# The start of a diffusion layer's first sub-layer: all of its scale and shift as products on TensorE in four column groups, with three ff tiles side by side

## The chip, the core and the metric

One core of a Trainium2 chip runs the whole layer. The metric is device microseconds of one execution; the kernel before takes 2782.91 us, the median of three runs (2781.95 to 2784.03). Engines are named as in the profile: PE is TensorE (PEld its weight loads), DVE is VectorE, ACT is ScalarE, POOL is GpSimd, SP is the engine whose queue issues most loads.

## The reference, cut to what matters

Two streams of 256 tokens (x, and the context ctx) of width 2048 pass a first feed-forward sub-layer, then token mixing, then (x alone) a second feed-forward sub-layer. The change lies in the start of the first sub-layer.

```python
mod   = (silu(c)     @ w_ada + b_ada)     # 9 chunks of 2048: shift, scale, gate of three sub-layers
mod_c = (silu(c_ctx) @ w_ada + b_ada)

def half_ffn(s, m, slot, g, w_up, w_down):
    h = rms_norm(s, g) * (1 + chunk(m, 3 * slot + 1)) + chunk(m, 3 * slot)
    return s + 0.5 * chunk(m, 3 * slot + 2) * swiglu(h, w_up, w_down)

x   = half_ffn(x,   mod,   0, g_norm[0], w_ffn1_up, w_ffn1_down)
ctx = half_ffn(ctx, mod_c, 0, g_norm[0], w_ffn1_up, w_ffn1_down)
```

All is float32. w_ada is 2048 x 18432; chunks 0 and 1 (shift and scale of the first sub-layer) are 33.6 MB of it. w_ffn1_up is 2048 x 11264.

## The kernel before, in words

Activations stand transposed: a d-tile is 128 of the 2048 columns on the partitions, by 256 tokens; there are 16 d-tiles, and x and ctx (the two halves, 0 and 1) lie in pairs of d-tiles. An ff tile is 128 of the 5632 hidden columns; there are 44. For one ff tile TensorE multiplies, over all 16 d-tiles, a gate part and an up part, each as three products of a high and a low part (`mm3`, lines 192 to 194): 96 products of 512 columns (both halves). The weights of a quarter of k (four d-tiles) of one ff tile are one load of 512 KB (`raw`), which ScalarE casts to the high part (`whi`, line 187) and VectorE or GpSimd subtracts to the low part (`wlo`, line 188). `close` forms silu(gate) * up (lines 287, 288).

The operand h of a d-tile needs three things: the inverse rms of both halves (lines 206 to 211, from sums of squares on TensorE, line 228), x scaled by it (GpSimd, line 404), and the d-tile's scale and shift for both conditioning vectors. `wave_h` (lines 393 to 395) then makes the high and low part of h.

Scale and shift come in two ways. `ada_dve` computes one chunk of one d-tile as dot products on VectorE (line 136): two loads of 512 KB (`adaw`), each against both conditioning rows `crow`, which TensorE broadcasts over the partitions beforehand (line 106). `ada_pe` does it on TensorE (line 157): silu(c) and silu(c_ctx) are two weight columns (`cs`), 256 columns of w_ada (scale and shift of one d-tile) are the moving operand, and 16 products add up over k into two rows; the rows are copied (line 159), turned into columns by two small products (line 162), and biased (line 165).

The order of all this is a list written by hand, `PLAN`: P is `ada_pe` of a d-tile (5 of the 16), D is `ada_dve` of one (10, and d-tile 0 ahead of the list), X is a scaling on GpSimd, H is `wave_h`, W and V are the products of one ff tile and one quarter of k, their weights split on GpSimd or VectorE. The k order of the first up projection is the order in which the H stand. Four ff tiles run side by side (`WAVE = 4`, eight PSUM banks). After them each ff tile runs alone, and 1.25 dot products for the remaining modulation (7 chunks) are put behind each quarter (`ada_hook`).

Each engine works through its instructions in a fixed order, which a scheduler makes of the program at build time. Loads go through the SP queue in order, the ones of `ada_dve` in this stretch through ScalarE's queue; a load waits in its queue until its buffer is free.

Of the kernel before, what the change touches and what calls it, by code (L numbers as in the profile page):

```python
# [13 lines left out]
AF = mybir.ActivationFunctionType  # L14
# [15 lines left out]
# order of the first sub-layer's start: P/D modulation of a d-tile on TensorE/VectorE, X normalised pair of  # L30
# d-tiles, H operand of a d-tile, W/V products of (ff tile, quarter of k), its weights split on GpSimd/VectorE
PLAN = (
    "X5 P11 P12 P13 X0 X6 X1 X2 H11 X3 X4 H0 D1 H1 X7 D4 H12 W00 D2 H4 W10 D3 P14 H3 W20 H2 D15 H15 W01 "
    "V11 P5 W21 H13 D7 W30 W31 D6 H6 H5 H14 D9 W02 H7 W12 W32 W22 D8 H8 H9 D10 H10 W03 W13 W33 W23"
).split()
KORD = [int(s[1:]) for s in PLAN if s[0] == "H"]
PE_D = sorted(int(s[1:]) for s in PLAN if s[0] == "P")
WAVE = 4
# [3 lines left out]
# steps of the query projection between those of the long convolution, and of the hyena gate in the attention  # L42
# [11 lines left out]
def hybrid_layer_kernel(ctx: ExitStack, tc: tile.TileContext, a):  # L54
# [39 lines left out]
    # ------------------------------------------------------- inputs, silu(c)  # L94
    cs = cload("cs", (P, KT, 2))
    S.activation(cs, cs, AF.Silu)
    adap_cm = tc.tile_pool(name="adap", bufs=2)
    adap = adap_cm.__enter__()
    crow = [T(adap, (P, D), f"crow{i}", bufs=1) for i in range(2)]
    for b in range(2):  # L100
        for i in range(2):
            r = T(adap, (1, D // 2), "adaw", bufs=4)
            nc.sync.dma_start(r, a["crow"][i : i + 1, b * (D // 2) : (b + 1) * (D // 2)])
            for q in range(2):
                ps = PB()
                PE.matmul(ps, ones[0:1, :], r[:, q * 512 : (q + 1) * 512], start=True, stop=True)
                S.activation(crow[i][:, b * (D // 2) + q * 512 : b * (D // 2) + (q + 1) * 512], ps, AF.Silu)
# [7 lines left out]
    # ------------------------------------------------------- adaLN modulation  # L115
# [8 lines left out]
    def ada_dve(c, d, b, eng=None):  # L124
# [23 lines left out]

    def ada_pe(d):
        """scale and shift of one d-tile of the first sub-layer, as rows on TensorE."""  # L150
        row = PB((2, 2 * P))
        for kp in range(8):
            t = U((P, 2, 2 * P))
            nc.sync.dma_start(t, a["w_ada1"][PE_D.index(d), kp])
            for k2 in range(2):
                k = kp * 2 + k2
                PE.matmul(row, cs[:, k, :], t[:, k2, :], start=k == 0, stop=k == KT - 1)
        rows = tmp2((2, 2 * P))
        S.copy(rows, row)
        col = PB((P, 2, 2))  # L160
        for j in range(2):
            PE.transpose(col[:, j, :], rows[:, j * P : (j + 1) * P], ident[0:2, 0:2])
        for i in range(2):
            for j, c in ((0, 1), (1, 0)):
                V.tensor_add(mod[i][c][:, d : d + 1], col[:, j, i : i + 1], bada[:, c * KT + d : c * KT + d + 1])
        ada_finish(1, d, d + 1)

    # ------------------------------------------------------------- primitives
# [27 lines left out]
    def mm2(ps, w, x, start, stop):  # L196
        """x [P, 2, L]: hi and lo side by side; so are the two sums in ps, to be added up by the reader"""
# [19 lines left out]
    def rstd_steps(pairs, n, y, on_pe=False):  # L217
        """y [P, L] = 1 / rms over partitions and tiles of pairs ([P, 2, L] each), on every partition."""
# [23 lines left out]
    def modulated(i, d, rs, cm, hi, lo):  # L242
        """hi + lo = x * rs * scale + shift for token part i, d-tile d."""
# [19 lines left out]
    class Ffn:  # L263
# [12 lines left out]
        def piece(self, j, kq, ps2, eng=None):  # L276
            whi, wlo = weight(self.wup[j, kq], (P, 4, 2, P), eng)
            for k4 in range(4):
                k = kq * 4 + k4
                for half in range(2):  # L280
                    self.mm(ps2[half], (whi[:, k4, half, :], wlo[:, k4, half, :]), self.h[k], k == 0, k == KT - 1)
            self.hook()

# [21 lines left out]
        def down(self, g, parts=None, last=None):  # L305
            """adds group g's share to y; parts: token parts (all at once if None); last(i, d, ps) ends a column."""
# [31 lines left out]
        def most(self, first):  # L338
            """all but the last group's down projection, which follows one ff tile behind"""
# [5 lines left out]
    # ------------------------------------------------------------------ ffn 1  # L345
# [11 lines left out]
    def regate():  # L357
        """the gates have come: x returns and takes y times gate, tile by tile"""
# [27 lines left out]
    ada_finish(1, 0, 1)  # L386

    def wave_h(d):
# [595 lines left out]
```

## Time and profile before

| | |
|---|---|
| runs, median (lowest to highest) | 2782.91 us (2781.95 to 2784.03) |
| profiled execution, first to last instruction | 2780.1 us, mean granted clock 0.988 |
| busy: PE, DVE, ACT, POOL | 97%, 71%, 36%, 11% of the span |
| first 206.1 us: PE, DVE busy | 170.25 us, 183.12 us |
| 260 to 1500 us: PE busy | 1240.00 of 1240.00 us |
| loads in the first 206.1 us | 248 GB/s on average |

A row of groups gives line, engine, operation, tiles (out<-in), shape and count, then busy us, mean ns of one, and idle time of the engine just before with what ended it. A row of the timeline gives start and duration in us. A busy PE is not PE at its peak: matmul records overlap, so the step from one start to the next says more than a record's length. An fp32 product is two records, and two weight loads.

### The profile page before, as it was taken

The page shows a single profiled execution, that of the slowest core. Times are in us where ns is not written, and L with a number is a line of the kernel's source. Part 1 is how long each engine was busy: PE and PEld are TensorE (multiplying, and loading weights), DVE is VectorE, ACT ScalarE, POOL GpSimd, SP SyncE. Part 2 cuts the span into 40 slices and gives each one's busy share as a digit, 9 for nine tenths or more (in the row PEclk, how much of TensorE's full clock was granted, in tenths as well). Part 3 has the DMA queues.
Part 4 walks back from the last instruction along what each step waited for, and adds up shares of the span by engine and source line. Part 5 has one row for each costly group of instructions (what it writes and reads, how often), then busy time and mean ns, then how long its engine had stood idle before and what let it go on. Part 6 is the DMA issues. An engine that isn't in the chain of part 4 may idle for free. (4 is left out here: it accounts for less than half of the span.)

```text
span 2780.1 us, 34758 instructions
## 1 busy us (share of the span) xinstructions
PE 2701.8 (97%) x13160; PEld 2232.5 (80%) x13160; DVE 1968.8 (71%) x3126; ACT 992.6 (36%) x1354; POOL 305.0 (11%) x143
## 2 busy tenths in 40 slices
PE   7889999999999999999999999988999999999999
PEld 3568888888888888887777878777878888888888
DVE  6999998986686666525353696878666666666666
ACT  3343222222222222222332455355454444444443
POOL 4320000000000000000000530232101111111111
PEclk9999999999999999999999999999999999999999
DMA  8756666565686666422222345233545555555554
GB/s 290 261 195 236 231 215 220 207 233 207 239 297 220 214 212 221 145 99 95 90 91 84 129 167 190 99 107 112 194 153 186 188 182 183 188 182 183 188 185 172
DMA packets 147814, 506.64 MB, mean 182 GB/s; under 512 B 17563, under 2 KB 19772, under 8 KB 147648
## 3 DMA queue, kind: packets, MB, share of 16 engines
q1 hardware_dynamic: 141744, 482.94, 49.8%
q10 hardware_dynamic: 5904, 21.50, 2.2%
q8 instruction: 103, 1.69, 0.2%
q14 instruction: 63, 0.52, 0.1%
HBM read 502.28 MB, written 2.10 MB: 181 GB/s over the span
## 5 line engine op out<-in xcount | busy, mean ns | idle before, releaser
L187 ACT CAST whi<-raw 128x1024 fp32r<-128x1024 f32 x648 | 681.9, 1053 | 1295.5 <-PE pa L193 468.5
L188 DVE TENSOR_TENSOR wlo<-raw,whi 128x1024 fp32r<-128x1024 f32 x557 | 686.8, 1234 | 452.3 <-ACT whi L187 438.3
L200 PE MATMUL pa<-u,whi 128*128 128x512 f32 x2016 | 715.2, 401 | 10.3 <-DVE u L248 5.9
L202 PE MATMUL pa<-u,wlo 128*128 128x256 f32 x1890 | 533.1, 282 | 2.9 <-POOL wlo L188 1.9
L192 PE MATMUL pa<-u,whi 128*128 128x512 f32 x1344 | 525.3, 392 | 9.1 <-ACT u L393 7.6
L193 PE MATMUL pa<-u,whi 128*128 128x512 f32 x1344 | 524.5, 390 | 3.1 <-DVE u L395 2.8
L194 PE MATMUL pa<-u,wlo 128*128 128x512 f32 x1344 | 524.0, 390 | 3.0 <-POOL wlo L188 3.0
L188 POOL TENSOR_TENSOR wlo<-raw,whi 128x1024 fp32r<-128x1024 f32 x91 | 231.8, 2549 | 2210.4 <-ACT whi L187 2189.3
L200 PEld LDWEIGHTS pa<-u,whi 128*128 128x128 f32 x2016 | 377.9, 189 | 98.2 <-issue 6.3
L202 PEld LDWEIGHTS pa<-u,wlo 128*128 128x128 f32 x1890 | 359.7, 190 | 7.4 <-POOL wlo L188 2.3
L192 PE MATMUL pb<-u,whi 128*128 128x512 f32 (+1 forms) x832 | 313.6, 377 | 3.2 <-DVE u L548 2.3
L194 PE MATMUL pb<-u,wlo 128*128 128x512 f32 (+1 forms) x832 | 312.2, 376 | 3.4 <-DVE wlo L188 2.5
L193 PE MATMUL pb<-u,whi 128*128 128x512 f32 (+1 forms) x832 | 312.1, 375 | 0.0
L192 PEld LDWEIGHTS pa<-u,whi 128*128 128x128 f32 x1344 | 252.9, 188 | 69.5 <-ACT u L393 9.4
L193 PEld LDWEIGHTS pa<-u,whi 128*128 128x128 f32 x1344 | 252.9, 188 | 57.4 <-DVE u L395 5.1
L136 DVE CUSTOM_DVE_ANT_0 adas<-adaw,crow,mod 128x1024 bf16<-128x1024 f32 x204 | 277.0, 1358 | 30.0 <-DMA adaw<-in_w_adaT_dram 22.9
L194 PEld LDWEIGHTS pa<-u,wlo 128*128 128x128 f32 x1344 | 252.9, 188 | 56.5 <-POOL wlo L188 3.9
L136 DVE CUSTOM_DVE_ANT_0 adas<-adaw,crow,bada 128x1024 bf16<-128x1024 f32 x204 | 273.3, 1340 | 29.3 <-DMA adaw<-in_w_adaT_dram 26.6
L200 PE MATMUL pb<-u,whi 128*128 128x512 f32 x736 | 250.4, 399 | 2.3 <-DVE u L321 2.3
L192 PEld LDWEIGHTS pb<-u,whi 128*128 128x128 f32 x832 | 158.5, 191 | 35.0 <-ACT whi L187 4.8
L194 PEld LDWEIGHTS pb<-u,wlo 128*128 128x128 f32 x832 | 158.5, 191 | 31.8 <-DVE wlo L188 2.7
L193 PEld LDWEIGHTS pb<-u,whi 128*128 128x128 f32 x832 | 158.6, 191 | 27.8 <-issue 0.4
(196 smaller groups left out, 2367.8 us busy)
## 6 DMA issues: line engine op xcount, KB each, us to landing
raw<-in_w_up_dram SPq DMA_DIRECT2D x352, 512.0 KB, 3.6
adaw<-in_w_adaT_dram SPq DMA_DIRECT2D x227, 512.0 KB, 4.9
raw<-in_w_dn_dram SPq DMA_DIRECT2D x184, 512.0 KB, 3.5
adaw<-in_w_adaT_dram ACTq DMA_DIRECT2D x41, 512.0 KB, 5.3
raw<-in_w_hy_dram SPq DMA_DIRECT2D x32, 512.0 KB, 3.4
raw<-in_w_o_dram SPq DMA_DIRECT2D x32, 512.0 KB, 3.5
u<-in_w_ada_dram SPq DMA_DIRECT2D x40, 256.0 KB, 5.6
raw<-in_w_kv_dram SPq DMA_DIRECT2D x16, 512.0 KB, 3.5
```

Source lines behind the costliest of these rows:

```text
L136: V.tensor_tensor_reduce(out=sc, in0=t, in1=crow[i][:, b * (D // 2) : (b + 1) * (D // 2)], scale=1.0, scalar=mcol if b else bada[:, n : n ...
L187: S.copy(hi, raw)
L188: (eng or V).tensor_sub(lo, raw, hi.bitcast(F32))
L192: PE.matmul(ps, w[0], xx[0], start=start, stop=False)
L193: PE.matmul(ps, w[0], xx[1], start=False, stop=False)
L194: PE.matmul(ps, w[1], xx[0], start=False, stop=stop)
L200: PE.matmul(ps, w[0], x, start=start, stop=stop)
L202: PE.matmul(ps[:, 0, :], w[1], x[:, 0, :], start=False, stop=False)
```

## The change

Scale and shift of all 16 d-tiles are computed on TensorE. silu(c) and silu(c_ctx) are padded with zeros to 32 weight columns, and the 16 products over k go to four column groups of the array (partitions 0, 32, 64, 96 of one PSUM bank), k modulo 4. The copy to SBUF takes all 128 partitions, and the product that turns rows into columns has a matrix `sel` as moving operand, which adds the four groups. The loads are 1 MB each (eight k at once) into a pool `rowp` of four buffers, all on the SP queue. Bias and norm gain are folded into one operation for the scale.

`PLAN` is gone: the d-tiles come in order, `ada_pe` two d-tiles ahead of `wave_h`. Three ff tiles run side by side; in the first quarter of k they take each d-tile as it comes, later a quarter at once. All weights are split on ScalarE and VectorE. The conditioning rows for the later dot products are loaded after the wave, by DMAs that broadcast them over the partitions, into memory that `rowp` has given back; the dot products begin with the fourth ff tile.

```diff
-WAVE = 4
+WAVE = 3
...
+    sel = T(const, (P, 2), "sel")
+    V.tensor_add(sel, ident[:, 0:2], ident[:, 32:34])
+    for g in (2, 3):
+        V.tensor_add(sel, sel, ident[:, 32 * g : 32 * g + 2])
+    cs = T(const, (P, KT, 32), "csp")
+    V.memset(cs, 0.0)
+    cs2 = cload("cs", (P, KT, 2))
+    S.activation(cs[:, :, 0:2], cs2, AF.Silu)
+    rowp_cm = tc.tile_pool(name="rowp", bufs=4)
...
     def ada_pe(d):
-        row = PB((2, 2 * P))
-        for kp in range(8):
-            t = U((P, 2, 2 * P))
-            nc.sync.dma_start(t, a["w_ada1"][PE_D.index(d), kp])
-            for k2 in range(2):
-                k = kp * 2 + k2
-                PE.matmul(row, cs[:, k, :], t[:, k2, :], start=k == 0, stop=k == KT - 1)
-        rows = tmp2((2, 2 * P))
-        S.copy(rows, row)
+        row = PB()
+        for kh in range(2):
+            t = T(rowp, (P, 8, 2 * P), "wrow")
+            nc.sync.dma_start(t, a["w_ada1"][d, kh])
+            for k8 in range(8):
+                k = kh * 8 + k8
+                g = 32 * (k % 4)
+                PE.matmul(row[g : g + 32, 0 : 2 * P], cs[:, k, :], t[:, k8, :], start=k < 4, stop=k >= KT - 4)
+        rows = tmp2((P, 2 * P))
+        S.copy(rows, row[:, 0 : 2 * P])
         col = PB((P, 2, 2))
         for j in range(2):
-            PE.transpose(col[:, j, :], rows[:, j * P : (j + 1) * P], ident[0:2, 0:2])
+            PE.matmul(col[:, j, :], rows[:, j * P : (j + 1) * P], sel, start=True, stop=True)
         for i in range(2):
-            for j, c in ((0, 1), (1, 0)):
-                V.tensor_add(mod[i][c][:, d : d + 1], col[:, j, i : i + 1], bada[:, c * KT + d : c * KT + d + 1])
-        ada_finish(1, d, d + 1)
+            V.scalar_tensor_tensor(mod[i][1][:, d : d + 1], col[:, 0, i : i + 1], bada1[:, d : d + 1], gn[:, 0, d : d + 1],
+                                   op0=ALU.add, op1=ALU.mult)
+            V.tensor_add(mod[i][0][:, d : d + 1], col[:, 1, i : i + 1], bada[:, d : d + 1])
...
+    def wave_x(q):
+        for i in range(2):
+            G.tensor_mul(xs[i][q], xs[i][q], rs[:, i : i + 1, :].broadcast_to((P, 2, L)))
...
-    wave = {}
-    for op in PLAN:
-        if op[0] == "P":
-            ada_pe(int(op[1:]))
...
-            f1.piece(j, kq, wave[j], G if op[0] == "W" else V)
+    wave = [f1.open(alt=j >= 2) for j in range(WAVE)]
+    ahead = 2
+    for d in range(ahead):
+        ada_pe(d)
+    for kq in range(4):
+        w = {}
+        for k4 in range(4):
+            d = kq * 4 + k4
+            if d % 2 == 0:
+                wave_x(d // 2)
+            wave_h(d)
+            if d + ahead < KT:
+                ada_pe(d + ahead)
+            if kq == 0:
+                for j in range(WAVE):
+                    if k4 == 0:
+                        w[j] = weight(f1.wup[j, 0], (P, 4, 2, P))
+                    f1.tile(d, k4, w[j], wave[j])
+            elif k4 == 3:
+                for j in range(WAVE):
+                    f1.piece(j, kq, wave[j])
     for j in range(WAVE):
         f1.close(j, wave[j])
+    rowp_cm.__exit__(None, None, None)
+    adap_cm = tc.tile_pool(name="adap", bufs=2)
+    adap = adap_cm.__enter__()
+    crow = [T(adap, (P, D), f"crow{i}", bufs=1) for i in range(2)]
+    for i in range(2):
+        nc.sync.dma_start(crow[i], a["crow"][i : i + 1, :].partition_broadcast(P))
+        S.activation(crow[i], crow[i], AF.Silu)
     f1.hook = ada_hook
```

What the scheduler makes of it, at three places (L numbers are lines of the kernel that the rows are from; numbers behind a tile's name count tiles). First PE, where the modulation of a d-tile (L157 before, L151 now, with the small products L162 and L156) meets the first products of the ff tiles (L192 to L194 before, L186 to L188 now). Before:

```order
L157 MATMUL pb_365<-u_386,cs_74 2x256 x2
L157 MATMUL pb_365<-u_390,cs_74 2x256 x2
L157 MATMUL pb_365<-u_394,cs_74 2x256 x2
L192 MATMUL pa_507<-u_417,whi_511 128x512
L193 MATMUL pa_507<-u_418,whi_511 128x512
L194 MATMUL pa_507<-u_417,wlo_512 128x512
L162 MATMUL pb_400<-ident_67,sg_398 128x2 x2
L192 MATMUL pa_508<-u_417,whi_511 128x512
```

Now, in the first quarter of k (wrow_384 is the second half of d-tile 3's weights, u_365 is h of d-tile 1):

```order
L188 MATMUL pa_226<-u_365,wlo_344 128x512
L186 MATMUL pb_227<-u_365,whi_355 128x512
L187 MATMUL pb_227<-u_366,whi_355 128x512
L151 MATMUL pb_373<-wrow_384,csp_78 32x256 x8
L188 MATMUL pb_227<-u_365,wlo_356 128x512
L186 MATMUL pb_228<-u_365,whi_355 128x512
L187 MATMUL pb_228<-u_366,whi_355 128x512
L156 MATMUL pb_396<-sel_74,sg_394 128x2 x2
L188 MATMUL pb_228<-u_365,wlo_356 128x512
L186 MATMUL pa_223<-u_423,whi_331 128x512
```

Before, three d-tiles' modulation stood together ahead of the first ff product, and a whole quarter of one ff tile followed; now half a d-tile's modulation stands between ff products of three ff tiles. d-tiles 6 to 9 stand together, ahead of the second quarter. Second SP, around the loads of the second quarter's ff weights. Before:

```order
L154 DMA u_390<-in_w_ada_dram 128x512
L154 DMA u_394<-in_w_ada_dram 128x512
L182 DMA raw_509<-in_w_up_dram 128x1024
L182 DMA raw_575<-in_w_up_dram 128x1024
L182 DMA raw_685<-in_w_up_dram 128x1024
L182 DMA raw_757<-in_w_up_dram 128x1024
```

Now (wrow_662 and wrow_672 are d-tile 9, wrow_792 begins d-tile 10, wrow_870 d-tile 12):

```order
L147 DMA wrow_662<-in_w_ada_dram 128x2048
L147 DMA wrow_672<-in_w_ada_dram 128x2048
L176 DMA raw_691<-in_w_up_dram 128x1024
L176 DMA raw_721<-in_w_up_dram 128x1024
L176 DMA raw_751<-in_w_up_dram 128x1024
L147 DMA wrow_792<-in_w_ada_dram 128x2048
L147 DMA wrow_802<-in_w_ada_dram 128x2048
L147 DMA wrow_830<-in_w_ada_dram 128x2048
L147 DMA wrow_840<-in_w_ada_dram 128x2048
L176 DMA raw_937<-in_w_up_dram 128x1024
L176 DMA raw_967<-in_w_up_dram 128x1024
L176 DMA raw_997<-in_w_up_dram 128x1024
```

The ff weights now stand in one queue with all loads of w_ada, three behind every four d-tiles or so. Third ACT at the end of the wave. Before (sq_1261 belongs to the h of the last d-tile, sg_1387 and sg_1394 are gates, whi_1359 weights of the wave's last product):

```order
L394 ACTIVATE sq_1261<-u_154,mod_0_20_118,mod_1_22_120 128x256
L393 ACTIVATE u_1259<-u_182,mod_0_21_119,mod_1_23_121 128x256
L394 ACTIVATE sq_1261<-u_182,mod_0_21_119,mod_1_23_121 128x256
L287 ACT_TABLE_LOAD
L287 ACTIVATE sg_1387<-pa_507 128x512
L187 CAST whi_1359<-raw_1357 128x1024
L287 ACTIVATE sg_1394<-pa_573 128x512
```

Now (u_1115 is h of d-tile 15, whi_1125 the first weights of the last quarter, sg_1213 the gate of the first ff tile, whi_1248 the first weights of the fourth):

```order
L391 ACTIVATE u_1115<-u_119,mod_0_8_90,mod_1_10_92 128x256
L392 ACTIVATE sq_1117<-u_119,mod_0_8_90,mod_1_10_92 128x256
L391 ACTIVATE u_1115<-u_135,mod_0_9_91,mod_1_11_93 128x256
L392 ACTIVATE sq_1117<-u_135,mod_0_9_91,mod_1_11_93 128x256
L181 CAST whi_1125<-raw_1123 128x1024
L181 CAST whi_1155<-raw_1153 128x1024
L181 CAST whi_1185<-raw_1183 128x1024
L426 ACT_TABLE_LOAD
L426 ACTIVATE crow_241_1238<-crow_241_1238 128x2048
L426 ACTIVATE crow_242_1239<-crow_242_1239 128x2048
L283 ACTIVATE sg_1213<-pa_223 128x512
L181 CAST whi_1248<-raw_1246 128x1024
```

Before, the gates of the wave followed the last h directly, and the rows had been made at the very start. Now the casts of the last quarter stand behind the last h, and the two Silu of the conditioning rows ahead of the gates.

More of the change, by code (lines that the diff above doesn't have):

```diff
@@ L29 @@
 EPS = 1e-6
[L32 to L37, printed above, removed]
-WAVE = 4
+WAVE = 3
 ADA_RATE = 1.25
@@ L92, in cload @@
         return t
[L95 to L107, printed above, removed]
+    sel = T(const, (P, 2), "sel")
[7 more added lines that the diff above has]
+    rowp_cm = tc.tile_pool(name="rowp", bufs=4)
+    rowp = rowp_cm.__enter__()
     bada = cload("bada", (P, 9 * KT))
@@ L278, in piece, with tile @@
             for k4 in range(4):
-                k = kq * 4 + k4
-                for half in range(2):
-                    self.mm(ps2[half], (whi[:, k4, half, :], wlo[:, k4, half, :]), self.h[k], k == 0, k == KT - 1)
+                self.tile(kq * 4 + k4, k4, (whi, wlo), ps2)
             self.hook()
+        def tile(self, k, k4, w, ps2):
+            for half in range(2):
+                self.mm(ps2[half], (w[0][:, k4, half, :], w[1][:, k4, half, :]), self.h[k], k == 0, k == KT - 1)
         def close(self, j, ps2):
@@ L373, in ada_hook @@
             ada_next()
-    for i, c in ((0, 1), (1, 0)):
-        for b in range(2):
-            ada_dve(c, 0, b, nc.sync)
+    for i in range(2):
         for q in range(KT // 2):
@@ L381, in hybrid_layer_kernel @@
             xs[i].append(t)
+    V.tensor_scalar(bada1, bada[:, KT : 2 * KT], 1.0, None, op0=ALU.add)
     f1 = Ffn(2, a["w_up1"], a["w_dn1"], 0)
@@ L914, in pcol, with pair @@
         return c_(v.reshape(-1, P).T)
-    def pair(w, ncol, order=None):
-        if order is not None:
-            w = w.reshape(KT, P, -1)[list(order)]
+    def pair(w, ncol):
         return c_(w.reshape(4, 4, P, 2, ncol, P).transpose(4, 0, 2, 1, 3, 5))
@@ L938, in _prepare @@
     d["w_adaT"] = c_(wa.T).reshape(9 * KT, P, D)
-    blocks = [np.concatenate([wa[:, o + b * P : o + (b + 1) * P] for o in (D, 0)], axis=1) for b in PE_D]
-    d["w_ada1"] = np.stack([w.reshape(8, 2, P, 2 * P).transpose(0, 2, 1, 3) for w in blocks])
+    blocks = [np.concatenate([wa[:, o + b * P : o + (b + 1) * P] for o in (D, 0)], axis=1) for b in range(KT)]
+    d["w_ada1"] = np.stack([w.reshape(2, 8, P, 2 * P).transpose(0, 2, 1, 3) for w in blocks])
     d["bada"] = pcol(i["b_ada"][0])
```

25 lines of the change are left out of this document (6 added, 19 removed).

## The prediction

> **What bounds the kernel now.** The page first: its busy times and its 40 slices of 69.5 us (the digits are busy tenths).
>
> ```profile
> PE 2701.8 (97%) x13160; PEld 2232.5 (80%) x13160; DVE 1968.8 (71%) x3126; ACT 992.6 (36%) x1354; POOL 305.0 (11%) x143
> PE   7889999999999999999999999988999999999999
> DVE  6999998986686666525353696878666666666666
> ```
>
> TensorE (PE) is the bound; its gaps lie in the first three slices, the place of the change, and around slice 27, which the change leaves alone. Next the table by stage (columns: window, its length, busy time and count of PE, PEld, DVE, ACT, POOL, then granted clock, DMA share, GB/s), the gate operation (Silu of a finished ff tile, L287) up to 300 us, and the products L192 in the first window, whose columns are PE and PEld alone.
>
> ```profile
> 0.00:206.10 206.10, 170.25 (x634) 107.82 (x635) 183.12 (x269) 75.58 (x124) 70.45 (x37) 0.93 0.71 248
> 206.10:260.00 53.90, 53.90 (x239) 44.66 (x238) 53.47 (x93) 19.88 (x38) 0.00 (x0) 1.00 0.72 244
> 260.00:1500.00 1240.00, 1240.00 (x5440) 1017.13 (x5439) 837.17 (x1346) 306.83 (x352) 0.00 (x0) 1.00 0.53 188
> L287 ACT ACTIVATE sg<-pb x2: 592/598/605, 205.6 to 206.1; 128x512 f32<-128x512 f32 x2
> 0.00:206.10 206.10, 51.38 (x128) 25.43 (x129) 0.93 0.71 248
> ```
>
> The wave of four ff tiles ends at 206.1 us; by then PE has made 3 x 128 = 384 products (L193 and L194 have the same count), exactly those four tiles. From there to 1500 us PE has no gap, and a product takes 1240/5440 = 0.228 us. So the question is one number: how early is the work of four tiles done? Four tiles are 384 x 0.228 = 87.6 us; the other 118.5 us are loss. A microsecond won there reaches the end, for nothing but PE's own work follows up to 1500 us and the code behind is unchanged.
>
> Why the loss? The groups of that window (busy us, mean ns | idle before):
>
> ```profile
> L136 DVE CUSTOM_DVE_ANT_0 adas<-adaw,crow,mod 128x1024 bf16<-128x1024 f32 x46 | 74.3, 1615 | 4.6 <-ACT crow L107 3.6
> L136 DVE CUSTOM_DVE_ANT_0 adas<-adaw,crow,bada 128x1024 bf16<-128x1024 f32 x46 | 70.7, 1537 | 10.4 <-DMA adaw<-in_w_adaT_dram 9.7
> L157 PE MATMUL pb<-u,cs 128*2 128x256 f32 x160 | 39.4, 404 | 3.5 <-DMA u<-in_w_ada_dram 3.4
> L228 PE MATMUL pb<-sq,ones 128*128 128x256 f32 x64 | 18.4, 444 | 1.1 <-ACT sq L225 1.1
> L187 ACT CAST whi<-raw 128x1024 fp32r<-128x1024 f32 x18 | 18.7, 1047 | 44.4 <-DMA u<-in_w_ada_dram 12.7 <-DMA adaw<-in_w_adaT_dram 10.7 <-DMA raw<-in_w_up_dram 5.6
> L393 ACT ACTIVATE u<-u,mod,mod 128x256 fp32r<-128x256 f32 x32 | 18.1, 594 | 31.6 <-DVE mod L136 30.8 <-DMA u<-in_w_ada_dram 0.7
> L159 ACT COPY sg<-pb 2x256 f32<-2x256 f32 x5 | 1.8, 363 | 18.7 <-DVE mod L136 12.5 <-DMA adaw<-in_w_adaT_dram 5.7 <-PE pb L157 0.5
> ```
>
> VectorE (DVE) is the limit of the start: 145 of its 183 busy us are dot products, and the wait that ends last for ScalarE's operands (L393) is on them, 30.8 us.
>
> **The change, part by part.**
>
> *Removed:* 88 of those 92 dot products (11 d-tiles x 8), the broadcast of the conditioning rows on PE, and the fourth tile of the wave. The fourth tile comes back afterwards as 96 x 0.228 = 21.9 us of pure PE time. So the wave of three must end by 206.1 - 21.9 = **184.2 us** to break even.
>
> *Added on PE:* 16 d-tiles instead of 5, each 16 fp32 products of 256 columns. The price of a d-tile is the term that decides. Rows of PE's timeline (start, duration):
>
> ```profile
> 48.62 7.07 PE L157 MATMUL pb<-u,cs 128*2 128x256 f32 x32
> 63.46 9.66 PE L157 MATMUL pb<-u,cs 128*2 128x256 f32 x32
> 87.56 0.39 PE L193 MATMUL pa<-u,whi 128*128 128x512 f32 x1
> 87.78 0.39 PE L194 MATMUL pa<-u,wlo 128*128 128x512 f32 x1
> 88.10 7.07 PE L157 MATMUL pb<-u,cs 128*2 128x256 f32 x32
> ```
>
> One d-tile is 32 records, two for each product, 7.07/32 = 0.22 us apart (9.66 us in all at a low clock). No row shows products on different column groups side by side, so I bound the price. Upper end: no overlap, 7.07 us. Lower end: all four groups at once, 7.07/4 = 1.77 us. I take the middle: records start in program order in every row, and the two records of a product go to the same group. The second must follow the first; only the first record of the next product can run beside it. That halves the time: **3.5 us**.
>
> The Trainium skill has a measured number for this: "TensorE: Matmul & The Clock Gate", Part 3 (Packing small matmuls), gives 2.38 times for three column tiles. By that a d-tile is 7.07/2.38 = 3.0 us and the sum below ends about 7 us earlier; no run here shows it, and it is not for two-record fp32 products.
>
> *Changing the shape of the array:* a product's record lasts 0.39 us while the next starts after 0.23 us. If the array must run empty at each change between 128 and 32 columns, that is 0.16 us, twice for each stretch of such products: 0.32 us (lower end: 0.09 us each way, by the step from 87.78 to 88.10). The upper end is what the Trainium skill states: by "TensorEngine Tiling (Array Packing)", Key Properties, a change of the tiling mode drains TensorE; no row here shows such a change.
>
> *Each d-tile's tail:*
>
> ```profile
> L162 PE MATMUL pb<-ident,sg 2*128 2x2 f32 x10 | 1.6, 232 | 11.6 <-ACT sg L159 11.6
> L165 DVE TENSOR_TENSOR mod<-pb,bada 128x1 f32<-128x1 f32 x20 | 1.8, 148 | 0.0
> ```
>
> PSUM copy (0.36 us by L159, wider now), two products whose weights are 128 columns of fp32, four small DVE operations of 0.15 us. The two products are bounded by 0.23 us (one L162 record) and by four records of L228, 4 x 0.44 = 1.8 us; I take half of that, 0.9 us. PE stands 1.7 us for copy and products where nothing is ordered between, about 0.9 us where ff products are.
>
> *Loads:* the same 33.6 MB of w_ada, now in 1 MB pieces on the SP queue alone, through four buffers; 4.2 MB of x and nine 0.52 MB weight loads up to the third quarter. The best rate, and rows for the start:
>
> ```profile
> 0.74 0.39 SPq L91 DMA_DIRECT2D cs<-in_cs_dram  x1
> 2.46 0.23 ACT L96 ACTIVATE cs<-cs 128x32 f32<-128x32 f32 x1 [0.44 <-DMA cs<-in_cs_dram]
> 15.00:20.00 5.00, 5.00 (x10) 2.87 (x10) 1.89 (x7) 2.34 (x4) 0.00 (x0) 1.00 1.04 401
> 40.00:45.00 5.00, 4.87 (x23) 1.98 (x22) 3.67 (x5) 0.42 (x1) 5.00 (x4) 1.00 1.04 400
> 38.24 12.96 POOL L404 TENSOR_TENSOR u<-u,u 128x512 f32<-128x512 f32 x8 [36.93 <-DVE u L211]
> 31.82 1.75 DVE L208 RECIPROCAL u<-u 128x256 f32<-128x256 f32 x1
> 34.59 0.42 DVE L209 TENSOR_TENSOR sg<-u 128x256 f32<-128x256 f32 x1
> ```
>
> At 400 GB/s a d-tile's 2.1 MB take 5.2 us, and all 42.5 MB up to the last d-tile 106 us. A PE that spends 3.5 us plus tail and ff products on a d-tile is the slower one.
>
> The sum, for a d-tile of 3.5 us:
> 1. A load issued at 0.74 is used at 2.46; x follows three small issues, so it lands from about 4.5 to 15 us (4.2 MB at 400 GB/s). The sums of squares occupy PE for 18.4 us, to about 23. The first half's rstd needs some 4 us of DVE (1.75 + 5 x 0.42) and is done near 18.5; GpSimd (POOL) scales eight tiles of the latent half and then the first of the context half, 9 x 1.62 = 14.6, to 33; operand h0 on ACT and DVE 2 us, to 35. PE meanwhile needs 23 + 3 x (3.5 + 1.7) less the last overlap = **38**.
> 2. First quarter, three tiles by d-tile: 72 x 0.228 = 16.4, d-tiles 3 to 5 10.5, tails 3, eight shape changes 2.6: **70.5**.
> 3. d-tiles 6 to 9 stand together in PE's order: 4 x (3.5 + 1.7) + a cast (1.05) = 21.8: **92.3**.
> 4. Second quarter, 72 products: **108.7**.
> 5. Third quarter with d-tiles 10 to 13: 16.4 + 14 + 3.6 + 2: **144.7**.
> 6. d-tiles 14 and 15: 9: **153.7**. The chain to the last quarter: copy 0.4, column 0.9, modulation 0.6, four activations of 0.59, the cast 1.05 behind them on ACT: 5.5: **159.2**.
> 7. Last quarter 16.4 + 1: **176.6**.
>
> That is 7.6 us before break-even. The profiled execution took 2780.1 us from first to last instruction, and the runs' median is 2782.9 us, so the launch adds 2.8 us to both kernels: 2782.9 - 7.6 = **2775 us**, 0.27% faster.
>
> *The wait that is added:*
>
> ```profile
> L107 ACT ACTIVATE crow<-pb 128x512 f32<-128x512 f32 x8 | 4.8, 598 | 9.3 <-PE pb L106 9.3
> L188 DVE TENSOR_TENSOR wlo<-raw,whi 128x1024 fp32r<-128x1024 f32 x3 | 3.6, 1216 | 0.0
> ```
>
> The conditioning rows now come by DMA after the last d-tile's products and pass ACT as two Silu of 128x2048 (four times L107's 0.60 us each, 2.4). Behind them on ACT stand the gates of the three tiles and the cast for tile 3; behind the first dot products on DVE its low half. The 2 MB land near 162, Silu ends by 167, two dot products by 171 (1.6 us each at most, plus the low half before it is needed). The last quarter's 16.4 us of PE work cover it until 176.6. Without that cover PE would stand for what is left, at most the whole 12 us from 159 to 171.
>
> GpSimd's weight splits move to DVE at 1.22 us each; freed of dot products it has room: nine ahead of the last quarter are 11 us.
>
> **The rivals.**
> - *Column groups run one after another* (slower). Place: the d-tiles on PE; price 7.07 instead of 3.5 us, on 16 of them 57 us; the wave ends at 233.7, 49.5 us past break-even: **2832 us**. For it: the L157 rows never show two records begun closer than 0.22 us. Against: their products all wrote the same columns. It turns to a loss from 4.0 us per d-tile on (7.6/16 = 0.5 us more).
> - *All four groups at once.* 1.77 us per d-tile saves 13 x 1.73 = 22.5 us on d-tiles 3 to 15 and 3 us ahead of them (POOL's 35 then sets step 1); the 26.7 MB up to d-tile 9 are there by 4.5 + 67 = 71, still ahead of PE. The wave ends at 151: **2750 us**. For it: eight products of a half carry one semaphore update, nothing separates them but order.
> - *Loads bind.* The first window moved 248 GB/s on average. At that rate 42.5 MB take 171 us, the last d-tile lands at 176, and products, chain and last quarter add 25: 201, 17 us late: **2800 us**. For it: the four buffers come free only through PE's products. Against, the longest hold of the SP queue in that window was for GpSimd's weight splits, which go:
>
> ```profile
> SPq L182 <- POOL wlo L188: 77.7, 12, 14.4
> ```
>
>
> **How the numbers follow.** Forecast 0.5, four at once 0.2, one after another 0.2, loads 0.1. What this kernel can tell from no change is about 0.2%, 5.6 us (2777.3 to 2788.5). The forecast's own range is 2765 to 2787 (first product, tails, shape changes: about 3 to 4 us each), so it gives faster 0.62, same 0.33, slower 0.05. Faster: 0.31 + 0.2 = 0.51, with a little from the loads 0.52; same 0.18; slower 0.03 + 0.2 + 0.07 = 0.30. The range reaches from just under the four-at-once case, 2747, to beyond the loads' case, 2812; only the serial case lies outside.
>
> **What would show it.** In the changed kernel's trace: a half d-tile (16 records) in about 1.75 us against 3.5 or 0.9; the first ff product near 38; the gate of the third tile near 177 (break-even 184); DVE idle for most of that time; PE without a gap from the last quarter on. The forecast is wrong if the records stand 0.22 us apart without overlap, if PE's waits in that stretch are on wrow loads, or if PE stands behind the conditioning rows' Silu.

## The result, and the profile after

The changed kernel takes **2758.66 us** (median of four runs, 2755.95 to 2761.21), the kernel before 2783.0 (four runs beside it): a ratio of 0.9912, 95% interval 0.9898 to 0.9926. That is faster, the side that the forecast took, and 16 us below its 2775; it lies inside the range (2747 to 2812), 9 us from the rival "all four groups at once". The profiled execution took 2754.2 us against 2780.1.

The page first: busy times, and TensorE and VectorE in 40 slices of 68.9 us.

```profile
PE 2687.7 (98%) x13550; PEld 2236.1 (81%) x13550; DVE 1844.0 (67%) x2982; ACT 993.1 (36%) x1359; POOL 257.5 (9%) x128
PE   8899999999999999999999999988999999999999
DVE  3298999866777575425443797878666666666666
```

VectorE's first slice has gone from 6 to 3: the dot products have left the start. Now the gate of the third ff tile (the end of the wave), and the table by stage, cut at the steps of the prediction (window, length, then busy us and count of PE, PEld, DVE, ACT, POOL, granted clock, DMA share, GB/s):

```profile
L283 ACT ACTIVATE sg<-pb x1: 599/599/599, 158.0 to 158.0; 128x512 f32<-128x512 f32 x1
0.00:39.30 39.30, 26.55 (x173) 17.96 (x173) 12.83 (x26) 19.87 (x35) 19.81 (x21) 0.91 0.93 360
39.30:66.30 27.00, 27.00 (x181) 17.74 (x180) 7.67 (x18) 9.24 (x17) 3.12 (x2) 0.94 0.76 278
66.30:84.00 17.70, 11.81 (x147) 6.46 (x146) 4.67 (x20) 10.49 (x21) 0.00 (x0) 0.89 1.00 402
84.00:102.00 18.00, 18.00 (x76) 14.30 (x76) 7.11 (x10) 6.08 (x8) 0.00 (x0) 0.92 0.74 306
102.00:129.20 27.20, 27.20 (x221) 18.55 (x220) 5.71 (x21) 10.75 (x21) 0.00 (x0) 1.00 0.90 352
129.20:139.00 9.80, 5.02 (x74) 2.92 (x73) 2.39 (x11) 5.79 (x12) 0.00 (x0) 0.96 0.52 187
139.00:158.00 19.00, 18.96 (x70) 15.02 (x71) 15.58 (x22) 11.03 (x12) 0.00 (x0) 0.84 0.97 358
260.00:1500.00 1240.00, 1240.00 (x5436) 1016.05 (x5435) 812.03 (x1297) 305.55 (x349) 0.00 (x0) 1.00 0.53 182
```

The wave of three ends at 158.0, and break-even was 184.2: 26.2 us won. The two spans differ by 25.9, the medians by 24.3. Behind the wave TensorE runs without a gap up to 1500 us, as before. The gates behind it keep the distance: the one of the 41st ff tile stands at 1394.3 us, and at 1420.3 before. So the frame of the prediction holds: what is won at the end of the wave is the whole result.

The term that decides is a d-tile on TensorE. All 16 as one group up to 182 us (busy us, mean ns | idle before), one of them in the timeline, and a stretch of 0.06 us of the same d-tile:

```profile
L151 PE MATMUL pb<-wrow,csp 128*32 128x256 f32 x512 | 35.0, 407 | 3.2 <-DMA wrow<-in_w_ada_dram 3.1
69.70 1.93 PE L151 MATMUL pb<-wrow,csp 128*32 128x256 f32 x32
69.70 0.42 PE L151 MATMUL pb<-wrow,csp 128*32 128x256 f32 x4
```

32 records take 1.93 us, and four of them begin within 0.06 us: eight bursts of four, 0.22 us apart. Before, the same 32 records took 7.07 us.

And the waits that are left (timeline of PE; the bracket is the idle time before, and what ended it):

```profile
33.27 1.01 PE L156 MATMUL pb<-sel,sg 128*128 128x2 f32 x4 [5.20 <-ACT sg L153]
34.22 3.64 PE L151 MATMUL pb<-wrow,csp 128*32 128x256 f32 x32
75.60 1.07 PE L151 MATMUL pb<-wrow,csp 128*32 128x256 f32 x16 [1.36 <-DMA wrow<-in_w_ada_dram]
80.58 1.94 PE L151 MATMUL pb<-wrow,csp 128*32 128x256 f32 x16 [1.35 <-DMA wrow<-in_w_ada_dram]
138.97 0.80 PE L186 MATMUL pa<-u,whi 128*128 128x512 f32 x1 [3.42 <-ACT whi L181]
139.56 0.63 PE L187 MATMUL pa<-u,whi 128*128 128x512 f32 x1
145.07 0.40 PE L187 MATMUL pa<-u,whi 128*128 128x512 f32 x1
```

After each long wait the next records are long: the d-tile at 34.22 takes 3.64 us, and ff products 0.63 until 145.07, where they are back at 0.40. After several short ones too: half a d-tile takes 1.07 us at 75.60 and 1.94 at 80.58.

### The profile page after: what moved, and what is told of

Its sections match the earlier page's. It is cut to its first block, busy times and chain, and to the rows that moved or that the text cites. A ratio compares the mean times of both kernels' runs of the same rounds, so it can differ in the third digit from the quotient of the medians.

```text
span 2754.2 us, 35301 instructions
## 1 busy us (share of the span) xinstructions
PE 2687.7 (98%) x13550; PEld 2236.1 (81%) x13550; DVE 1844.0 (67%) x2982; ACT 993.1 (36%) x1359; POOL 257.5 (9%) x128
## 3 DMA queue, kind: packets, MB, share of 16 engines
q8 instruction: 107, 1.75, 0.3%
## 5 line engine op out<-in xcount | busy, mean ns | idle before, releaser
L182 DVE TENSOR_TENSOR wlo<-raw,whi 128x1024 fp32r<-128x1024 f32 x572 | 705.6, 1235 | 488.3 <-ACT whi L181 474.0
L194 PE MATMUL pa<-u,whi 128*128 128x512 f32 x2016 | 714.9, 400 | 10.5 <-DVE u L242 5.9
L186 PE MATMUL pa<-u,whi 128*128 128x512 f32 x1376 | 540.3, 393 | 3.4 <-ACT whi L181 3.4
L187 PE MATMUL pa<-u,whi 128*128 128x512 f32 x1376 | 538.0, 391 | 0.0
L188 PE MATMUL pa<-u,wlo 128*128 128x512 f32 x1376 | 537.6, 391 | 0.0
L194 PEld LDWEIGHTS pa<-u,whi 128*128 128x128 f32 x2016 | 377.9, 189 | 98.3 <-issue 6.3
L182 POOL TENSOR_TENSOR wlo<-raw,whi 128x1024 fp32r<-128x1024 f32 x76 | 189.8, 2497 | 2250.8 <-ACT whi L181 2232.0
L186 PEld LDWEIGHTS pa<-u,whi 128*128 128x128 f32 x1376 | 259.8, 189 | 63.2 <-ACT whi L181 7.3
L187 PEld LDWEIGHTS pa<-u,whi 128*128 128x128 f32 x1376 | 260.0, 189 | 55.4 <-issue 2.1
L188 PEld LDWEIGHTS pa<-u,wlo 128*128 128x128 f32 x1376 | 259.1, 188 | 56.2 <-DVE wlo L182 1.9
L186 PE MATMUL pb<-u,whi 128*128 128x512 f32 (+1 forms) x800 | 300.1, 375 | 2.3 <-DVE u L556 2.3
L188 PE MATMUL pb<-u,wlo 128*128 128x512 f32 (+1 forms) x800 | 299.1, 374 | 2.5 <-DVE wlo L182 2.5
L187 PE MATMUL pb<-u,whi 128*128 128x512 f32 (+1 forms) x800 | 298.8, 374 | 0.0
L194 PE MATMUL pb<-u,whi 128*128 128x512 f32 x736 | 250.3, 399 | 2.3 <-DVE u L317 2.3
L126 DVE CUSTOM_DVE_ANT_0 adas<-adaw,crow,bada 128x1024 bf16<-128x1024 f32 x160 | 205.1, 1282 | 21.5 <-DMA adaw<-in_w_adaT_dram 17.3
L126 DVE CUSTOM_DVE_ANT_0 adas<-adaw,crow,mod 128x1024 bf16<-128x1024 f32 x160 | 205.1, 1282 | 18.0 <-DMA adaw<-in_w_adaT_dram 15.0
L186 PEld LDWEIGHTS pb<-u,whi 128*128 128x128 f32 x800 | 152.0, 190 | 32.8 <-ACT whi L181 4.8
L188 PEld LDWEIGHTS pb<-u,wlo 128*128 128x128 f32 x800 | 152.1, 190 | 29.2 <-DVE wlo L182 2.7
L187 PEld LDWEIGHTS pb<-u,whi 128*128 128x128 f32 x800 | 152.1, 190 | 26.4 <-issue 0.4
```

The costliest lines, as they stand in the source:

```text
L126: V.tensor_tensor_reduce(out=sc, in0=t, in1=crow[i][:, b * (D // 2) : (b + 1) * (D // 2)], scale=1.0, scalar=mcol if b else bada[:, n : n ...
L182: (eng or V).tensor_sub(lo, raw, hi.bitcast(F32))
L186: PE.matmul(ps, w[0], xx[0], start=start, stop=False)
L187: PE.matmul(ps, w[0], xx[1], start=False, stop=False)
L188: PE.matmul(ps, w[1], xx[0], start=False, stop=stop)
L194: PE.matmul(ps, w[0], x, start=start, stop=stop)
```

## Experiments

Theory: the price of a d-tile on TensorE, set by how many column groups run side by side, made the result. Rivals: the dot products' going is enough by itself; the groups alone are enough; the loads set the pace.

| kernel | d-tile us | last gate of the wave | time us | ratio to before (95%) |
|---|---|---|---|---|
| changed kernel | 1.93 | 158.0 | 2758.66 | 0.9912 (0.9898 to 0.9926) |
| one group | 7.09 | 215.0 | 2814.55 | 1.0115 (1.0099 to 1.0130) |
| two groups | 3.65 | 166.9 | 2765.25 | 0.9940 (0.9923 to 0.9956) |
| four groups, k in blocks | 4.59 | 192.2 | 2791.72 | 1.0032 (1.0020 to 1.0044) |
| before, with groups only | – | 210.8 | 2789.16 | 1.0021 (1.0011 to 1.0030) |
| each d-tile as it comes | 1.93 | 152.4 | 2758.14 | 0.9909 (0.9895 to 0.9924) |
| added products | 1.93 | 159.0 | 2759.46 | 0.9914 (0.9898 to 0.9931) |
| as it comes, early loads | 1.93 | 156.3 | 2763.55 | 0.9929 (0.9914 to 0.9944) |
| as it comes, rows later | 1.93 | 153.3 | 2751.59 | 0.9886 (0.9870 to 0.9903) |
| the same, added products | 1.93 | 150.7 | 2749.01 | 0.9880 (0.9866 to 0.9895) |

### One group, two groups

```diff
-                g = 32 * (k % 4)
+                g = 0
```

(with start and stop, the copy and the summing product cut to the rows in use; for two groups the line reads g = 32 * (k % 2))

> The changed kernel, but all 16 products of a d-tile go to the first column group: 32 rows, one after another; the copy and the small products take those 32 rows alone. Same operations, loads and plan otherwise. Theory (the column groups are what pays, through the price of a d-tile): 32 records 0.22 us apart, 7.07 us a d-tile in place of 1.93; 13 to 16 d-tiles lie on TensorE's path, 13 x 5.1 = 67 to 16 x 5.1 = 82 us at most, less the 15 to 20 us in which TensorE now waits for loads or runs at half clock: the wave of three ends between 210 and 235 us, 2805 to 2835 us, slower than the kernel before. Rival (dropping the dot products is what pays, and the groups matter little because the start hides them): wave end within 5 us of 158, 2757 to 2765.

> The changed kernel, but the 16 products of a d-tile alternate between two column groups (64 rows). It gives the price that the forecast assumed for a d-tile, so it tests the forecast's other steps. Theory: 3.5 to 3.7 us a d-tile (two side by side); by the forecast's sum the wave of three ends at 176.6 and the time is 2775; if the other steps of the sum were too dear as well (third gate at 158 with 1.93 us, 13 d-tiles x 1.7 = 22 us more), 170 to 180, 2768 to 2778. Rival (TensorE has slack in the start, so the price of a d-tile matters only partly): wave end under 165, below 2766.

One group (a d-tile, and the window up to the end of the wave), then rows of the version with two:

```profile
88.13 7.09 PE L151 MATMUL pb<-wrow,csp 128*32 128x256 f32 x32
0.00:215.00 215.00, 207.91 (x927) 128.37 (x928) 52.23 (x118) 73.91 (x125) 23.31 (x22) 1.00 0.67 241
```

```profile
40.22 0.50 PE L186 MATMUL pa<-u,whi 128*128 128x512 f32 x1
72.10 3.65 PE L151 MATMUL pb<-wrow,csp 128*32 128x256 f32 x32
76.75 3.65 PE L151 MATMUL pb<-wrow,csp 128*32 128x256 f32 x32
90.24 0.50 PE L186 MATMUL pa<-u,whi 128*128 128x512 f32 x1 [0.45 <-ACT whi L181]
107.53 3.65 PE L151 MATMUL pb<-wrow,csp 128*32 128x256 f32 x32
142.27 3.65 PE L151 MATMUL pb<-wrow,csp 128*32 128x256 f32 x32
140.00:160.00 20.00, 20.00 (x123) 13.57 (x122) 3.85 (x12) 9.61 (x14) 0.00 (x0) 1.00 0.57 205
```

With one group the kernel loses 32 us to the one before, inside what was expected: without column groups the change would have been a mistake, so the rival "the dot products' going is enough" falls. This version keeps all the rest of the change (three ff tiles, the new order, the loads on one queue); these parts were not tried one by one. From one group to two the wave wins 48.1 us, 14 times the 3.44 us that a d-tile got cheaper: some 14 of the 16 d-tiles lie on the path. From two to four it wins only 8.9, 5 times the 1.72 us. Where the rest went is in the windows up to the end of the wave, two groups and then four:

```profile
0.00:167.00 167.00, 156.27 (x927) 102.14 (x928) 52.55 (x118) 73.72 (x125) 23.90 (x22) 0.99 0.82 310
```

```profile
0.00:158.00 158.00, 134.53 (x926) 92.94 (x927) 55.98 (x127) 73.25 (x125) 22.93 (x22) 0.92 0.86 332
```

The same products keep TensorE busy 21.7 us less, but it stands 23.5 us instead of 10.7, and its clock falls from 0.99 to 0.92. The expected 170 to 180 was missed on the low side; the rival's bound for the time (2766) was met and its bound for the wave (165) was not.

### k in blocks

```diff
-                g = 32 * (k % 4)
-                PE.matmul(row[...], ..., start=k < 4, stop=k >= KT - 4)
+                g = 32 * (k // 4)
+                PE.matmul(row[...], ..., start=k % 4 == 0, stop=k % 4 == 3)
```

> The changed kernel, but k is dealt to the column groups in blocks of four (0 to 3 to the first group, and so on) in place of in turn; the same products, records and groups. Theory (records start in program order, and a record waits for the one before it in its own group): neighbours in the order share a group, so only the step from one block to the next overlaps: 6 to 7 us a d-tile, wave end 205 to 235, 2800 to 2832. Rival (TensorE reorders among groups, order does not matter): 1.93 us a d-tile and 2757 to 2762, as the changed kernel.

One d-tile whole, then stretches of 0.81 and 0.10 us of it:

```profile
30.15 4.59 PE L151 MATMUL pb<-wrow,csp 128*32 128x256 f32 x32
30.15 1.05 PE L151 MATMUL pb<-wrow,csp 128*32 128x256 f32 x4
31.04 0.62 PE L151 MATMUL pb<-wrow,csp 128*32 128x256 f32 x4
```

Neither: 4.59 us. The first four records go one at a time; from 31.04 they go in pairs, and the four in the third row are two pairs 0.22 us apart. No row names a record's group, but a group's eight records need eight such steps, so at 31.04 the first group is at its fifth, and what begins beside it must be the second group's first, the ninth in program order; the sixth to the eighth still wait. A step is (7.09 - 0.38)/31 = 0.216 us by the d-tile of one group. With four records ahead like this at each change of group a d-tile has 20 steps: 19 x 0.216 + 0.38 = 4.48 us. With k in turn, the four records that begin together must be the first, third, fifth and seventh, and the seventh too passes three that wait. So records do overtake each other between groups. Both orders fit one rule: a record begins when its group is free and at most three before it still wait. Other orders were not tried. Dealing k out in turn is worth 4.59 - 1.93 = 2.7 us per d-tile, here 33 us of run time.

### The groups alone

The kernel before, with plan, four ff tiles and dot products as they were; only the five d-tiles that TensorE computed there use four groups.

```diff
-        row = PB((2, 2 * P))
+        row = PB()
...
-                PE.matmul(row, cs[:, k, :], t[:, k2, :], start=k == 0, stop=k == KT - 1)
+                g = 32 * (k % 4)
+                PE.matmul(row[g : g + 32, 0 : 2 * P], cs[:, k, :], t[:, k2, :], start=k < 4, stop=k >= KT - 4)
```

> The kernel before, with its plan, its four ff tiles and its dot products, but the five d-tiles that TensorE computes there take four column groups (padded weights, 128-row copy, the small products with the summing matrix). Theory (VectorE's dot products set the start before): TensorE is freed by 5 x 5.1 = 26 us and only waits longer; the wave of four ends within 3 us of 206, 2778 to 2786, same. Rival (the groups alone bring it): up to 26 us earlier, down to 2757.

Windows to 211 us, this kernel and then the one before, each with VectorE's wait for the sums of squares:

```profile
0.00:211.00 211.00, 161.26 (x645) 107.56 (x646) 182.61 (x281) 75.17 (x125) 66.43 (x37) 0.85 0.71 245
DVE sg L213 <- PE pb L235: 11.7, 2, 8.1
```

```profile
0.00:211.00 211.00, 175.15 (x656) 111.90 (x657) 188.02 (x278) 78.35 (x128) 70.45 (x37) 0.93 0.72 251
DVE sg L206 <- PE pb L228: 7.1, 2, 3.9
```

TensorE is busy 14 us less and nothing comes of it: VectorE sets the end of that start. The kernel is even 6 us slower, which was not expected; its last gate comes 4.7 us later (210.8 for 206.1). VectorE stands 4.6 us longer for the sums of squares, which come late from TensorE: eight of their records begin at 40.44 us here and at 36.61 before. Just ahead of them TensorE stands 5.1 us in three waits for w_ada loads here, and 2.5 us in one before, and the eight take 3.78 us for 2.67. Its mean clock is 0.85 against 0.93. How much the order, these waits and the clock each do was not tried apart. So neither half of the change wins alone: groups without the dot products' going cost 6 us, their going without groups 32, both together win 24.

### Can the rest be had?

```diff
-            if kq == 0:
-                for j in range(WAVE):
-                    ...
-            elif k4 == 3:
-                for j in range(WAVE):
-                    f1.piece(j, kq, wave[j])
+            for j in range(WAVE):
+                if k4 == 0:
+                    w[j] = weight(f1.wup[j, kq], (P, 4, 2, P))
+                f1.tile(d, k4, w[j], wave[j])
```

> The changed kernel, but the three ff tiles take each d-tile as it comes in all four quarters of k, not in the first alone. The same products, loads and copies. In the changed kernel, d-tiles 6 to 9 stand together on TensorE (66 to 84 us, 17.6 us for four, 3.1 of them waits for loads, and then 6.8 us at half clock), and 14 and 15 before the last quarter (9.8 us, 3.4 of them a wait for the cast, then 6.8 us at half clock). Theory (those blocks leave TensorE thin while the loads stop at other times): with 18 products between d-tiles a d-tile takes about 4.1 + 1.9 + 0.8 us, the waits and the half clock there go, 8 to 13 us: the third gate at 145 to 150, 2745 to 2751. Rival (the loads set the pace on the whole): 42.5 MB arrive no sooner, third gate within 3 us of 158, 2756 to 2762.

The third gate, PE's first row behind it, and ScalarE's rows there (L422 is the Silu of the conditioning rows):

```profile
L283 ACT ACTIVATE sg<-pb x1: 597/597/597, 152.4 to 152.4; 128x512 f32<-128x512 f32 x1
156.35 0.76 PE L186 MATMUL pa<-u,whi 128*128 128x512 f32 x1 [3.32 <-ACT whi L181]
152.94 1.90 ACT L422 ACTIVATE crow<-crow 128x2048 f32<-128x2048 f32 x1
155.25 1.04 ACT L181 CAST whi<-raw 128x1024 fp32r<-128x1024 f32 x1
```

The wave does end 5.6 us earlier, which is not the 145 to 150 that was expected, and the time is the same. The gain is given back at once (the fourth ff tile's gate stands at 179.6 us, and at 179.7 in the changed kernel): the cast for the fourth ff tile stands on ScalarE behind the second Silu of the conditioning rows, TensorE waits 3.32 us, and then starts at half clock (a record of 0.76 us). The cast's weights are not late, for their load was issued at 127.28 us. It is the wait that the prediction named and found covered. In the changed kernel the cover is there, in this one it is not. None of TensorE's waits is for a w_ada load here, so these loads are not what holds it.

Next, the clock. This kernel adds products to the changed one that nobody reads:

```diff
+    KEEP = {0: (1, 0), 1: (12, 0), 7: (2, 0), 8: (2, 2), 9: (2, 2), 14: (2, 0), 15: (2, 8)}
+    def keep(row, d, n):
+        for _ in range(KEEP.get(d, (0, 0))[n]):
+            PE.matmul(row[:, 2 * P : 4 * P], ones, cs[:, 0:8, :], start=True, stop=True)
```

> The changed kernel with 34 products added on TensorE whose result nobody reads (ones by padded conditioning columns, 128x256, into the unused half of the row's bank): 12 while d-tile 1's row copy is awaited, 1 to 10 at d-tiles 0, 7, 8, 9, 14 and 15, each about 0.43 us. They do nothing but keep TensorE busy. Theory (the half clock from 32 to 43, 80 to 87 and 138 to 145 us follows from TensorE standing, and costs about 0.2 us on each product in it): the clock stays at 1.00 and the third gate comes 3 to 9 us earlier, 2749.5 to 2756. Rival (the half clock lies beside waits for loads and ScalarE and costs nothing, or the extra products stand in the way): 2757 to 2764.

```profile
34.41 7.13 PE L145 MATMUL pb<-csp,ones 128*128 128x256 f32 x24 [4.77 <-ACT sg L159]
```

This run answers nothing about the price of the clock. The added products share a bank with the row and so waited for the same copy; twelve of them then stood on the path for 7.13 us. The end of the wave moved by only 1 us, so some 6 us came back; whether by the clock or by the other order of products this run cannot tell.

> As the run that takes each d-tile as it comes, and besides the ff weights of a quarter are requested two d-tiles ahead of their use and the first quarter's cast stands before the loop, so that the first ff products need not wait behind d-tile 2. Theory: the first ff product starts at 34 to 36 us in place of 39.3, no quarter waits for its cast; the third gate comes at 140 to 147, 2739 to 2748, faster than the run without it by 2 to 6 us. Rival (the start of the first product is not on the path, since the later d-tiles wait for loads): within 1.5 us of that run.

```profile
34.85 0.80 PE L192 MATMUL pa<-u,whi 128*128 128x512 f32 x1
PE pa L192 <- ACT u L397: 5.1, 6, 1.0
PE pa L192 <- ACT whi L187: 4.8, 1, 4.8
```

The first ff product starts 4.5 us earlier, as meant, but h of later d-tiles is then late on ScalarE (5.1 us), and the fourth tile's cast again stands behind the Silu (4.8 us). A miss.

So the last pair: each d-tile as it comes, with the cast ahead of the gates and the conditioning rows after the third quarter of the fourth tile; and the same with added products that write a bank of the wave instead (the last two lines of the diff, in the second of the pair alone).

```diff
+    f1.first[WAVE, 0] = weight(f1.wup[WAVE, 0], (P, 4, 2, P))
     for j in range(WAVE):
         f1.close(j, wave[j])
...
+    calls = []
+    def first_hook():
+        calls.append(1)
+        if len(calls) < 3:
+            return
+        for i in range(2):
+            nc.sync.dma_start(crow[i], a["crow"][i : i + 1, :].partition_broadcast(P))
+            S.activation(crow[i], crow[i], AF.Silu)
+        f1.hook = ada_hook
+    f1.hook = first_hook
...
+        for _ in range(11 if d == 1 else 0):
+            PE.matmul(wave[1][1][:, 0, :], ones, cs[:, 0:8, :], start=True, stop=True)
```

> As the run that takes each d-tile as it comes, with the end of the wave changed: the fourth ff tile's first cast is made ahead of the wave's gates, and the conditioning rows are requested and passed through Silu only after the third quarter of the fourth ff tile, so the dot products begin some 12 us later. In the run without it the third gate came at 152.4, 5.6 us before the changed kernel's, but TensorE then stood 3.3 us for a cast that was behind the rows' Silu on ScalarE, and the fourth tile began at half clock (3.4 us of it). Theory (the gain was given back there): third gate at 152 to 153, no wait behind it, 2758.1 less 3.3 and less 1.7 for the clock: 2751 to 2754.5. Rival (the time was lost elsewhere, for instance to the later dot products): 2757 to 2760.

> As the run with the rows later, and 11 products added on TensorE whose result nobody reads (ones by padded conditioning columns, into a bank that the wave overwrites later), around d-tiles 0 and 1, where TensorE stands 5.2 us for d-tile 1's row copy at 28 to 33 us. Unlike in the first run with added products, they wait for nothing but TensorE itself. Theory (half clock from 33.5 to 43.8 follows from standing there): full clock from then on, d-tile 2 in 1.9 in place of 3.6 us, the first nine ff products 0.2 us shorter each, tails 0.4: third gate 3 to 5 us before that run's, 2747 to 2751. Rival (standing is not what sets the clock, or the added products delay the copy): no gain, within 1 us of that run or slower.

The version with the rows later: end of the wave, the fourth tile's cast, the window over it.

```profile
L284 ACT ACTIVATE sg<-pb x1: 597/597/597, 153.3 to 153.3; 128x512 f32<-128x512 f32 x1
150.97 1.06 ACT L181 CAST whi<-raw 128x1024 fp32r<-128x1024 f32 x1
140.00:160.00 20.00, 20.00 (x110) 15.59 (x103) 9.73 (x16) 13.08 (x17) 0.00 (x0) 1.00 0.73 267
```

No wait, full clock, 2751.59 us: 6.5 below the version without it, and 4.6 of that stand at the fourth tile's gate already (175.0 for 179.6). The gain was indeed given back behind the Silu; whether moving the cast or moving the rows would have done alone was not tried. With added products:

```profile
33.07 0.61 PE L158 MATMUL pb<-sel,sg 128*128 128x2 f32 x4 [2.30 <-ACT sg L153]
33.60 1.93 PE L151 MATMUL pb<-wrow,csp 128*32 128x256 f32 x32
39.92 1.22 PE L190 MATMUL pa<-u,wlo 128*128 128x512 f32 x2 [1.36 <-DVE wlo L184]
40.94 0.63 PE L188 MATMUL pa<-u,whi 128*128 128x512 f32 x1
```

d-tile 2 now takes 1.93 us where it took 3.64, and the third gate comes 2.6 us earlier (150.7). But the half clock only moved: the product at 40.94 takes 0.63 us, after TensorE has stood for the copy, a cast and a low half. The gate's gain falls short of the 3 to 5 us expected, and the two times, 2.6 us apart, have intervals that overlap: whether the added products pay is open.

The last version once more, beside the changed kernel on one chip:

> The changed kernel itself once more, beside the last version on the same chip, so that the two can be compared directly: 2756 to 2761.

> The version with each d-tile as it comes, the rows later and the added products around d-tiles 0 and 1, once more beside the changed kernel: 2747 to 2752, 7 to 11 us (0.25 to 0.4%) below it.

2759.56 us (2758.89 to 2762.03) and 2750.17 (2749.15 to 2751.29): 9.4 us apart, ranges clear of each other. So this version beats both kernels, at 0.988 of the one before.

## Why the prediction was right, and where its sizes were off

**The frame held.** VectorE set the start before (the groups alone won nothing), the fourth tile comes back as 22 us, break-even is 184.2, and a microsecond at the end of the wave is one in the time: the gate's 26.2, the spans' 25.9. (The launch is 1.8 us by the profiled execution, 2755.95 for a span of 2754.2, and not 2.8; it is in both kernels and changes nothing.)

**The sizes did not hold.** The forecast put the gain at 7.9 us, and it was 24.3. Its own range, 2765 to 2787, does not hold the result; the wide one does because it reached down to the rival at 2747. That "faster" came true says nothing for the price of a d-tile either: at the price that was put (the version with two groups) the kernel is faster too, because the other terms were too dear.

**The step that failed is the price of a d-tile: 3.5 us in the forecast, 1.93 measured.** The choice between the bounds of 1.77 and 7.07 rested on "records start in program order", with the second record of a product holding up the next group. The prediction's own sign told it first: half a d-tile takes 1.07 us, near the 0.9 of the rival and not 1.75. The run with k in blocks refutes the premise: a record passes up to three that wait when its group is free, which is just enough to put four groups side by side when k is dealt in turn. The Trainium skill, "TensorE: Matmul & The Clock Gate", Part 3 (Packing small matmuls), gives 2.38 times for three column tiles; it names no data type. Here two groups give 7.09/3.65 = 1.94 times and four 7.09/1.93 = 3.67, with two records per product; the Trainium skill's figure was nearer than the forecast's, and it was set aside.

**The other terms were too dear too.** The version with two groups has the forecast's price (3.65) and its wave ends at 166.9, not 176.6. By its rows: first ff product 40.2 for 38; first quarter 31.9 us for 32.5; d-tiles 6 to 9 18.1 for 21.8, since a tail costs 1.0 us (72.10 to 76.75, less 3.65) where 1.7 was put; second quarter 17.3 for 16.4; third 34.7 for 36; and from d-tile 14 to the end 24.6 for 31.9. There the forecast had TensorE standing through a chain of 5.5 us; in the window from 140 to 160 us it is busy without a gap, with ff products beside the chain. So of the 16 us between forecast and result some 10 are these terms, and 6.6 (2765.25 to 2758.66) the step from two groups to four.

**"All four at once" had the mechanism** and said 2750. In the changed kernel's stages its sum is missed by 4.3 us ahead of the first ff product (39.3 for 35: TensorE waits 5.2 us for d-tile 1's copy, which stands on ScalarE behind the first h, and that waits for d-tile 0's modulation on VectorE and then for GpSimd's scaling), 2.8 at d-tiles 6 to 9 (loads, 3.1 us of waits), and 1.6 each in the second and last quarter (half clock); the other stages are 3.4 us shorter than it says. So the rival "loads bind" is right about one stretch of 18 us (402 GB/s in the third window), and there alone.

**Changing the shape of the array** was put at 0.32 us per stretch. Two rows of the changed kernel around one, and the one behind:

```profile
45.93 0.39 PE L186 MATMUL pa<-u,whi 128*128 128x512 f32 x1
46.25 1.07 PE L151 MATMUL pb<-wrow,csp 128*32 128x256 f32 x16
47.25 0.50 PE L187 MATMUL pa<-u,whi 128*128 128x512 f32 x1
47.59 0.40 PE L188 MATMUL pa<-u,wlo 128*128 128x512 f32 x1
```

From the first of these to the last start 1.66 us pass. Two steps of ff products (0.23 each) and four bursts of the half d-tile (0.216 each) make 1.32 of them. So a stretch costs 0.34 us, in three parts: the steps into it, out of it and behind the next ff product are all longer. This term was right.

**The added wait** is hidden, as predicted, though everything comes 20 us earlier than put:

```profile
L426 ACT ACTIVATE crow<-crow x2: 1897/1904/1911, 142.1 to 143.9; 128x2048 f32<-128x2048 f32 x2
```

Both Silu run at 142 to 146, under a last quarter that lasts to 158. The price without the cover (at most 12 us) was 3.3 and 4.8 us, each with a slow start behind it, in the two versions where it was gone.

**One after another** was priced at 2832; the one-group version takes 2814.55. Its d-tile is the 7.07 us assumed; the wave ends at 215.0 instead of 233.7, by the same overpriced terms.

## What to carry to other kernels

A small product's price in column groups depends on the order in which the groups are served: deal them out in turn, and measure one d-tile before costing a plan with it. When a chain is shortened, look first at what stands on the off-path engines just behind its end: a Silu that was well hidden took back all of the next 5 us. Freeing an engine that nobody waits for wins nothing and may lose: here the end of the wave came 4.7 us later, for reasons that were not told apart.

## What the runs showed that was not expected

- Records of different column groups overtake each other: one passes up to three that wait (4.59 us for k in blocks; four starts within 0.06 us for k in turn).
- TensorE's granted clock halves after it has stood, and also where it is only thin: in the stage from 66.3 to 84 us no single wait is above 1.4 us, but PE is busy 11.81 of 17.70 us, and at its end half a d-tile takes 1.94 us for 1.07. The Trainium skill, "TensorE: Matmul & The Clock Gate", Part 1 (The HAM clock gate), puts the halving after an idle window of some 3.4 us. The wait of 5.20 us agrees with that, with the clock at half from 32.3 us, 4.2 us into it. The other two do not: from 80.2 us the clock is at half though TensorE was busy 1.68 of the 3.40 us before, and from 138.2 us, 2.6 us into the wait of 3.42, though it was busy 0.61 of the 3.40 before.
- Slower products can keep the clock: with one group the clock is 1.00 in all of the wave, with two 0.99, with four 0.92. Part of what a cheaper product saves is lost that way; how much was not measured cleanly.
- The changed kernel scatters more than the others: its runs lie between 2755.95 and 2762.03 us, and the end of its wave at 158.0 in one profile and 162.0 in another. Of these 4 us, 2.3 stand ahead of its first d-tile already (25.52 for 23.18).
- Versions that differ in the start alone drift apart once more far behind it: with k in blocks the gate of the 41st ff tile is 34.2 us later than in the changed kernel (1428.5 for 1394.3), and the end 37.1. Of the 6.9 us that the groups alone lose to the kernel before by the profiled executions, 2.2 arise there too. This is not explained.
